# A decoder layer on one core: x is transposed unscaled and its row factors multiply each projection; the recurrence's group norm is applied on ScalarE

## The chip, the cores and the metric
The kernel runs on one core of a Trainium2 chip. A core has five engines that each work through a queue of their own, in order: TensorE (PE, with its weight loads PEld), VectorE (DVE), ScalarE (ACT), GpSimd (POOL) and SyncE (SP, which issues DMAs here). They wait for each other by semaphores. The metric is the time of one execution in microseconds (us); lower is better.

## The reference, cut to what matters
One layer over 512 positions of 2048 channels. The first norm, the input projection and the group norm are what the change touches:

```python
h = rms_norm(x, norm_g[i])              # x / sqrt(mean(x*x) + eps) * g, per position
z = jnp.einsum('btd,dn->btn', h, w_in[i])   # r, k, v, two LoRA inputs | gate | pool input | pool gate
...
zs = zs + (token_shift(zs) - zs) * mu[i]
...
y = wkv7_scan(rh, wh, kh, vh, kk, ah)   # delta-rule recurrence over time, 16 heads of 64
y = head_group_norm(y, ln_w[i], ln_b[i])    # (y - mean) * rsqrt(var + eps) per head, then w and b
y_rwkv = (y + bonus) * silu(g_rwkv)
```

Beside it a pool group takes trailing means of its projection columns; both are joined, projected by w_out, added to x, gated by a second projection (w_pg), and normed.

## The kernel before, in words
Everything is f32, and each large product is made of three fp32r products: an operand is split into a rounded part and the rest (hi and lo: `whi`, `wlo` for weights, `hhi`, `hlo` for the normed x), and PE adds hi*hi, hi*lo and lo*hi (`mm3`, called through `mm`, L157 in the profile). Of a split, ACT makes hi by a copy and DVE makes lo by a subtraction (`wsplit`, L132 and L133; `split`, L137 and L138).

The opening (L255 to L313): x comes in four tiles of 128 positions. For each tile `stats` makes sums of squares (ACT and DVE in turns, L256 and L258), a root and a reciprocal (L262, L263), and scales the tile in place (L267, L269). Then `xt_half` transposes the tile by 128 columns on PE (L285) into a small PSUM buffer (six of them, from two pools), and evicts it twice with the norm's weight: hi on ACT (L286), lo on DVE (L287). The columns of the two LoRA inputs (`zl`) are projected at once, in two halves (`z_half`), since all else in the first head waits for them.

Then PE works through a stream of projections, 128 output columns at a time, in an order that is written out (`jobs`, `stream`): k, r, v, gate of a head, and pool units (`pool_unit`) between. Each unit is 16 x 3 products of 128x512 in one PSUM tile (`zcols`); its weights come in four chunks of four (`raw`, split by ACT and DVE). A finished k, r or v goes through the token shift (`shifted`: ACT L369, DVE L370), a gate through a silu (`silu2`), a pool input `u` is copied by ACT (L412). The stream is also the filling for the recurrence: whenever the recurrence of a pair of heads has a chain of small steps, `pump(n)` puts n products of the stream between them. PE keeps the program's order there (`pin`).

For each of 8 pairs of heads j: `decay_and_rate` makes the decay from the LoRA inputs (products pu and pa, tanh, a scan along time, two exponentials `pw` and `ipw`); `norm_key` and `scale_key` make normed keys (product `pss`, a DVE reciprocal); `prepare` makes the operands `ar` and `bk`; `scores` multiplies them (pm); `invert` solves small triangular systems; `gather` collects the chunks' operands (transposes `pbk` copied by ACT to `bkn`, L700, product pmv); `recur` steps over eight chunks: py, zs, pu (to `uv` on ACT, L797), ps, and the new state `sbd` on DVE (L809). At its end the outputs (`ysb`, 128 positions x 8 groups of 64) get their group norm: statistics, a reciprocal root by Newton steps on DVE, and eight DVE operations of 128x64 that subtract the mean and multiply (L854). `finish`, some time later, transposes them (pyt) and applies weight, bias, bonus and gate (L863). The preparation of the next pair, its `gather` included, stands between.

A scheduler decides where each engine's instructions stand in its queue; only PE's order is pinned.

Of the kernel before, what the change touches and what calls it, by code (L numbers as in the profile page):

```python
# [9 lines left out]
F32 = mybir.dt.float32  # L10
# [5 lines left out]
P = 128  # L16
T = 512
# [17 lines left out]
def trunk_kernel(ctx: ExitStack, tc: tile.TileContext, x, p, norm_g, w_in, mu, w0, w_up, a0, a_up,  # L35
# [20 lines left out]
    def load_x(tt, parts):  # L56
        xt = xp.tile([P, D], F32, name=f"xt{tt}", tag="xt")
        w_ = D // parts
        for i in range(parts):
            nc.sync.dma_start(out=xt[:, i * w_:(i + 1) * w_], in_=x[tt * P:(tt + 1) * P, i * w_:(i + 1) * w_])  # L60
        xs.append(xt)

    load_x(0, 4)
# [26 lines left out]
    nc.gpsimd.memset(seg.rearrange("p (c t) -> p c t", t=C)[:, :, 0:1], 0.0)  # L90

# [96 lines left out]
    LORD = (2, "l", "l", "l", "l", 3)  # L188
# [46 lines left out]

    for step in LORD:
        if step == "l":
            load_l()
        else:
            load_x(step, 2)  # L240
# [6 lines left out]
    WPOS, SPOS = (5, 7, 9, 11), (5, 10)  # L247

    def stats(tt, parts=2):
        w_ = D // parts  # L250
        ss = xp.tile([P, parts], F32, name=f"ss{tt}", tag="ss")
        for i in range(parts):
            cs = slice(i * w_, (i + 1) * w_)
            junk = xp.tile([P, w_], F32, name=f"junk{tt}_{i}", tag=f"junk{i % 2}", bufs=2)
            if i % 2 == 0:  # L255
                nc.scalar.activation(junk, xs[tt][:, cs], AF.Square, accum_out=ss[:, i:i + 1])  # L256
            else:
                nc.vector.scalar_tensor_tensor(junk, xs[tt][:, cs], 1.0, xs[tt][:, cs], ALU.mult, ALU.mult,  # L258
                                               accum_out=ss[:, i:i + 1])
        rs = xp.tile([P, 1], F32, name=f"rs{tt}", tag="rs")  # L260
        nc.vector.tensor_reduce(rs, ss, mybir.AxisListType.X, ALU.add)
        nc.scalar.activation(rs, rs, AF.Sqrt, bias=epsr, scale=1.0 / D)  # L262
        nc.vector.reciprocal(rs, rs)  # L263
        for i in range(4):
            cs = slice(i * D // 4, (i + 1) * D // 4)
            if i % 2 == 1:
                nc.scalar.activation(xs[tt][:, cs], xs[tt][:, cs], AF.Copy, scale=rs)  # L267
            else:
                nc.vector.tensor_scalar(xs[tt][:, cs], xs[tt][:, cs], rs, None, ALU.mult)  # L269

    stats(0, 4)
# [3 lines left out]
    stats(1, 4)  # L275
# [19 lines left out]
    wl_ = []  # L295
    for d in range(KT):
        xt_half(0, d)
        if d in WPOS:
# [5 lines left out]
        if d in SPOS:  # L304
            stats(2 + SPOS.index(d))
# [875 lines left out]
```

## Time and profile before

| | us |
|---|---|
| three runs | 1095.40, 1096.56, 1097.19; median 1096.56 |
| span of the profiled execution | 1095.9, 0.66 below the median |
| PE busy | 1070.8 |
| DVE busy | 708.2 |
| ACT busy | 448.3 |
| first product of k0 (end of the opening) | starts at 35.83 |
| first scores, pm(0) | start at 75.47 |

The durations of the profile are those of single instructions; since an engine begins the next one before the last has ended, the time that each one costs in a dense row is the distance from start to start, which is shorter. A row of a timeline can hold several like instructions (x4); its length is then that of the whole run. "Idle before <-" names what ended an idle time.

### The profile page before, as it was taken

How to read it: one execution, taken by the hardware profiler on the slowest of the kernel's cores; microseconds unless marked ns; L12 is line 12 of the kernel's file. 1: busy time of each engine (PE TensorE's matmuls, PEld its weight loads, DVE VectorE, ACT ScalarE, POOL GpSimd, SP SyncE). 2: the span in 40 equal slices, each digit the busy share in tenths (PEclk: the TensorE clock that was granted, in tenths of full speed). 3: DMA queues.
4: the chain of work that ended last, by engine and by line, in shares of the span. 5: the costliest groups of instructions: out<-in, count | busy, mean ns of one | idle time of the engine just before them, and what ended most of it. 6: DMA issues, size and time to landing. Idle time of an engine off the chain costs nothing.

```text
span 1095.9 us, 17196 instructions
## 1 busy us (share of the span) xinstructions
PE 1070.8 (98%) x6060; PEld 877.6 (80%) x6060; DVE 708.2 (65%) x1835; ACT 448.3 (41%) x917; POOL 76.9 (7%) x180
## 2 busy tenths in 40 slices
PE   5999999999999999999999999999999999999996
PEld 4888878887788888788878788888888888888885
DVE  6687867878688679678886956454433424445366
ACT  7633535345335335353343344543222222233337
POOL 2100110110110110100101101000000000000000
PEclk9999999999999999999999999999999999999999
DMA  7433433332423333333334242775534438455534
GB/s 233 116 96 97 111 92 84 96 100 73 120 82 105 104 92 89 96 82 93 91 94 119 79 138 93 232 233 169 172 124 136 167 99 244 137 189 137 181 106 154
DMA packets 178486, 138.56 MB, mean 126 GB/s; under 512 B 34678, under 2 KB 139743, under 8 KB 178399
## 3 DMA queue, kind: packets, MB, share of 16 engines
q1 hardware_dynamic: 157694, 103.89, 32.1%
q10 hardware_dynamic: 20704, 33.56, 9.8%
q8 instruction: 48, 0.79, 0.3%
q14 instruction: 40, 0.32, 0.1%
HBM read 118.02 MB, written 18.87 MB: 125 GB/s over the span
## 4 chain that ended last, share of the span: by engine, by line
PE 86%; DVE 5%; DMA 4%; ACT 3%; issue 1%; SPq 0%; ACTq 0%; DVEq 0%
PE acc_o L157 16%; PE zb L157 14%; PE acc_g L157 14%; PE zv L157 8%; PE zk L157 7%; PE zg L157 7%; PE zr L157 7%; PE py L157 2%; PE pple L157 2%; PE pm L157 1%; PE pu L157 1%; DMA n<-nd 1%; PE pp L157 1%; DMA raw_g<-in_w_pg_dram 1%; PE ps L157 1%
## 5 line engine op out<-in xcount | busy, mean ns | idle before, releaser
L133 DVE TENSOR_TENSOR wlo_g<-raw_g,whi_g 128x512 fp32r<-128x512 f32 x84 | 57.0, 685 | 79.6 <-ACT whi_g L132 76.5
L157 PE MATMUL zb<-hhi,whi_b 128*128 128x512 f32 x256 | 107.0, 418 | 0.0
L133 DVE TENSOR_TENSOR wlo_o<-raw_o,whi_o 128x512 fp32r<-128x512 f32 x64 | 43.9, 690 | 91.4 <-ACT whi_o L132 91.4
L157 PE MATMUL zb<-hhi,wlo_b 128*128 128x512 f32 x256 | 100.5, 393 | 0.0
L157 PE MATMUL acc_o<-whi_o,ylo 128*128 128x512 f32 x256 | 100.2, 391 | 0.0
L157 PE MATMUL acc_o<-whi_o,yhi 128*128 128x512 f32 x256 | 99.9, 390 | 0.0
L157 PE MATMUL zb<-hlo,whi_b 128*128 128x512 f32 x256 | 99.9, 390 | 0.0
L157 PE MATMUL acc_o<-wlo_o,yhi 128*128 128x512 f32 x256 | 99.8, 390 | 0.0
L132 ACT CAST whi_g<-raw_g 128x512 fp32r<-128x512 f32 x84 | 51.9, 620 | 102.7 <-PE acc_g L157 55.4
L157 PE MATMUL acc_g<-whi_g,x2hi 128*128 128x512 f32 x208 | 81.3, 391 | 0.0
L157 PE MATMUL acc_g<-wlo_g,x2hi 128*128 128x512 f32 x208 | 80.9, 389 | 0.0
L157 PE MATMUL acc_g<-whi_g,x2lo 128*128 128x512 f32 x208 | 80.7, 389 | 0.0
L132 ACT CAST whi_o<-raw_o 128x512 fp32r<-128x512 f32 x64 | 39.9, 623 | 97.0 <-PE acc_o L157 96.7
L816 POOL TENSOR_SCALAR s0p<-sbd,pw 64x64 f32<-64x64 f32 x96 | 56.6, 589 | 322.8 <-DVE sbd L809 255.0
L132 ACT CAST whi_b<-raw_b 128x512 fp32r<-128x512 f32 x64 | 39.7, 621 | 86.5 <-PE zv L157 35.4
L133 DVE TENSOR_TENSOR wlo_b<-raw_b,whi_b 128x512 fp32r<-128x512 f32 x64 | 43.8, 685 | 34.2 <-ACT whi_b L132 32.9
L157 PEld LDWEIGHTS zb<-hhi,wlo_b 128*128 128x128 f32 x256 | 48.0, 188 | 11.1
L661 DVE TENSOR_TENSOR xw<-xw,tm 128x60 f32<-128x60 f32 (+24 forms) x248 | 52.1, 210 | 6.8
L157 PEld LDWEIGHTS acc_o<-wlo_o,yhi 128*128 128x128 f32 x256 | 48.1, 188 | 10.3 <-DVE wlo_o L133 0.4
L157 PEld LDWEIGHTS acc_o<-whi_o,yhi 128*128 128x128 f32 x256 | 48.1, 188 | 9.7
L157 PEld LDWEIGHTS acc_o<-whi_o,ylo 128*128 128x128 f32 x256 | 48.1, 188 | 9.8
L157 PEld LDWEIGHTS zb<-hhi,whi_b 128*128 128x128 f32 x256 | 48.2, 188 | 8.5
(285 smaller groups left out, 2550.0 us busy)
## 6 DMA issues: line engine op xcount, KB each, us to landing
raw_b<-in_w_in_dram SPq DMA_DIRECT2D x64, 256.0 KB
raw_o<-in_w_out_dram SPq DMA_DIRECT2D x64, 256.0 KB
raw_g<-in_w_pg_dram SPq DMA_DIRECT2D x64, 256.0 KB
raw_k<-in_w_in_dram SPq DMA_DIRECT2D x32, 256.0 KB
raw_r<-in_w_in_dram SPq DMA_DIRECT2D x32, 256.0 KB
raw_v<-in_w_in_dram SPq DMA_DIRECT2D x32, 256.0 KB
raw_g<-in_w_in_dram SPq DMA_DIRECT2D x32, 256.0 KB
n<-nd SPq DMA_DIRECT2D x16, 256.0 KB
```

The costliest lines, as they stand in the source:

```text
L132: nc.scalar.copy(hi, raw)
L133: nc.vector.tensor_tensor(lo, raw, hi.bitcast(F32), ALU.subtract)
L157: i = nc.tensor.matmul(*a, **k)
L661: nc.vector.tensor_tensor(xw[:, 0:n_, s + 1:32], xw[:, 0:n_, s + 1:32], tm[:, 0:n_, 0:w_], ALU.add)
L816: nc.gpsimd.tensor_scalar(s0p[hc, :], nxt[hc, hc], pcn[hc], None, ALU.mult)
```

## The change
1. x's tiles are loaded in another order (0 and 1 in turns, then 2 and 3 in halves between the LoRA weights) and transposed as they are. `hhi` and `hlo` hold x times the norm's weight, without the row factor. The squares come later in the program; after the first two chunks of k0's projection (24 products, now ahead of all else) `roots` makes the 512 row factors, spreads them over all partitions by a product of a matrix of ones with four diagonal matrices, `prs`, and keeps them as `rsB` (128x512).
2. Every finished projection is multiplied by `rsB`: a DVE operation in PSUM (`by_row`) for k, r, v, the gates and `zl`; for `u` the product takes the place of ACT's copy.
3. In `decay_and_rate` the lower halves of the two LoRA products use the tiles `uhh` and `ahh` (whose lower halves now hold the rest of the split), so that the ACT casts into `uaz` and the tile `lal` go.
4. The group norm is applied on ACT, eight Identity activations with scale and bias from memory; DVE makes the bias (-mean * factor) in one small operation.

The core of the diff:

```diff
-    load_x(1, 4)
+    load_x(1, 0)
+    for i in range(1, 4):
+        for tt in range(2):
+            load_x(tt, i)
...
-    LORD = (2, "l", "l", "l", "l", 3)
+    LORD = ("l", 2, 3, "l", 2, 3, "l", "l")
...
-        for i in range(4):
-            cs = slice(i * D // 4, (i + 1) * D // 4)
-            if i % 2 == 1:
-                nc.scalar.activation(xs[tt][:, cs], xs[tt][:, cs], AF.Copy, scale=rs)
-            else:
-                nc.vector.tensor_scalar(xs[tt][:, cs], xs[tt][:, cs], rs, None, ALU.mult)
...
+    def roots():
+        rs = xp.tile([P, NT, 1], F32, name="rs", bufs=1)
+        nc.vector.tensor_reduce(rs, ssq_, mybir.AxisListType.X, ALU.add)
+        nc.scalar.activation(rs, rs, AF.Sqrt, bias=epsr, scale=1.0 / D)
+        nc.vector.reciprocal(rs, rs)
+        dg = xp.tile([P, NT, P], F32, name="dg", bufs=1)
+        for tt in range(NT):
+            nc.vector.tensor_scalar(dg[:, tt, :], ident, rs[:, tt, :], None, ALU.mult)
+        ps = psM.tile([P, T], F32, name="prs", tag="m")
+        mm(ps, ones, dg.rearrange("p a t -> p (a t)"), start=True, stop=True)
+        nc.scalar.copy(rsB, ps)
...
     for d in range(KT):
         z_half(1, d)
+        if d % CK == CK - 1 and d < 3 * CK:
+            ahead_k()
+        square(d // 4, d % 4)
+    pin[0] = True
+    begun = psA.tile([P, T], F32, name="zk0", tag="acc")
+    for c in range(BEGUN):
+        k_first(c)
+    roots()
...
+    nc.vector.tensor_tensor(zl, zl, rsB, ALU.mult)
     shifted(zl, la, 24)
...
+    def by_row(ps):
+        nc.vector.tensor_tensor(ps, ps, rsB, ALU.mult)
...
+                if kk == KT - 1 and scaled:
+                    by_row(ps)
                 yield 3
...
-            nc.scalar.copy(u_, ps)
+            nc.vector.tensor_tensor(u_, ps, rsB, ALU.mult)
...
-            nc.scalar.copy(z_[hi, :], raw[hi, :])
-            nc.vector.tensor_tensor(st[lo, :], raw[lo, :], st[lo, :].bitcast(F32), ALU.subtract)
+            nc.vector.tensor_tensor(z_[0:64, :], raw[0:64, :], st[0:64, :].bitcast(F32), ALU.subtract)
...
-        mm(ps, uaz[0], lal, start=False, stop=True)
+        mm(ps, uaz[0], uhh, start=False, stop=True)
...
+        nc.vector.scalar_tensor_tensor(nt8, mvr[:, :, 0:1], -1.0, rs8, ALU.mult, ALU.mult)
         for i in range(8):
-            nc.vector.tensor_scalar(y8[:, i, :], y8[:, i, :], mvr[:, i, 0:1], rs8[:, i, :],
-                                    ALU.subtract, ALU.mult)
+            nc.scalar.activation(y8[:, i, :], y8[:, i, :], AF.Identity, scale=rs8[:, i, :], bias=nt8[:, i, :])
```

The change moves instructions in the queues. In the rows below each instruction has its line, its operation, what it writes and reads, and the tile's size; the lines of the changed kernel are 3 to 32 higher.

DVE's queue at the start, before, from the end of the first tile's squares to the first evictions (`junk` are the squares, `rs` the row factor, `xt` the tile of x, `hlo` the eviction):

```order
L261 TENSOR_REDUCE rs_170<-ss_161 128x1
L263 RECIPROCAL rs_170<-rs_170 128x1
L269 TENSOR_SCALAR xt_78<-xt_78,rs_170 128x512 x2
L258 SCALAR_TENSOR_TENSOR junk_1_184,ss_181<-xt_85 128x512
L86 CAST blk<-blkf 128x128
L274 COPY ngc<-pt_prm 128x16
L258 SCALAR_TENSOR_TENSOR junk_3_188,ss_181<-xt_85 128x512
L261 TENSOR_REDUCE rs_190<-ss_181 128x1
L263 RECIPROCAL rs_190<-rs_190 128x1
L269 TENSOR_SCALAR xt_85<-xt_85,rs_190 128x512 x2
L287 SCALAR_TENSOR_TENSOR hlo<-pt_h_0_199,ngc,hhi 128x256
L287 SCALAR_TENSOR_TENSOR hlo<-pt_h_1_204,ngc,hhi 128x256
```

The same place in the changed kernel:

```order
L264 SCALAR_TENSOR_TENSOR junk_1_401,ssq__164<-xt_78 128x512
L89 CAST blk<-blkf 128x128
L281 COPY ngc<-pt_prm 128x16
L264 SCALAR_TENSOR_TENSOR junk_3_417,ssq__164<-xt_78 128x512
L264 SCALAR_TENSOR_TENSOR junk_1_427,ssq__164<-xt_79 128x512
L293 SCALAR_TENSOR_TENSOR hlo<-pt_h_0_169,ngc,hhi 128x256
L293 SCALAR_TENSOR_TENSOR hlo<-pt_h_1_174,ngc,hhi 128x256
L293 SCALAR_TENSOR_TENSOR hlo<-pt_h_2_179,ngc,hhi 128x256
```

The reductions, reciprocals and scalings are gone from the head of the queue; three squares of the first two tiles are left ahead of the first `hlo`, though the program writes them later.

DVE's queue ahead of the first scores, from a weight split of the gate to the last operand `bk` (`kk` keys, `kp` the other operand, `sv` the shifted v), before:

```order
L599 TENSOR_TENSOR kk_817<-kk_817,tha_844 128x512
L133 TENSOR_TENSOR wlo_g_3_777<-raw_g_3_774,whi_g_3_776 128x512
L370 SCALAR_TENSOR_TENSOR sv_933<-zv_801,prm,sv_933 128x511
L600 TENSOR_TENSOR bk_961<-kk_817,ipw_837 128x4x128
L601 SCALAR_TENSOR_TENSOR kp_962<-sr_798,dprm,kp_962 128x512
L133 TENSOR_TENSOR wlo_k_0_783<-raw_k_0_780,whi_k_0_782 128x512
```

The same place in the changed kernel:

```order
L139 TENSOR_TENSOR wlo_g_3_783<-raw_g_3_780,whi_g_3_782 128x512
L425 TENSOR_TENSOR zv_779<-zv_779,rsB 128x512
L630 TENSOR_TENSOR kk_795<-kk_795,tha_820 128x512
L632 SCALAR_TENSOR_TENSOR kp_939<-sr_776,dprm,kp_939 128x512
L398 SCALAR_TENSOR_TENSOR sv_910<-zv_779,prm,sv_910 128x511
L139 TENSOR_TENSOR wlo_k_0_789<-raw_k_0_786,whi_k_0_788 128x512
L631 TENSOR_TENSOR bk_938<-kk_795,ipw_813 128x4x128
```

The product of zv by `rsB` is new; `kp` and the split of `wlo_k_0` stood behind `bk` and now stand ahead of it.

ACT's queue at the gather for the second pair of heads, before (`pw`, `ipw` exponentials, `bkn` the copies of the operands, `uaz` the casts, `zs`, `mv` first chunk):

```order
L539 ACTIVATE pw_2386<-sig_2382 128x8x64
L132 CAST whi_b_2_1384<-raw_b_2_1382 128x512
L540 ACTIVATE ipw_2387<-sig_2382 128x512
L700 COPY bkn_2404<-pbk_0_2405 128x512
L700 COPY bkn_2404<-pbk_1_2411 128x512
L525 CAST uaz_570<-ur_2595 64x128
L524 CAST as_2602<-ar_2599 128x128
L525 CAST uaz_571<-ar_2599 64x128
L712 COPY zs_568<-pmv_2438 64x128
L713 COPY mv_2455<-pmv_2438 128x512
```

The same place in the changed kernel, where L886 is the group norm of the pair before:

```order
L570 ACTIVATE pw_2367<-sig_2363 128x8x64
L138 CAST whi_b_2_1388<-raw_b_2_1386 128x512
L886 ACTIVATE ysb_1642<-ysb_1642,nt_2329,rs_2326 128x64 x8
L571 ACTIVATE ipw_2368<-sig_2363 128x512
L731 COPY bkn_2385<-pbk_0_2386 128x512
L731 COPY bkn_2385<-pbk_1_2392 128x512
L743 COPY zs_599<-pmv_2419 64x128
L744 COPY mv_2436<-pmv_2419 128x512
```

The eight applies stand behind `whi_b_2` and ahead of `ipw` and both `bkn`; the two `uaz` casts are gone. The sixth pair's gather has the same order; at the others one or both `bkn` stand ahead of the applies.

More of the change, by code (lines that the diff above doesn't have):

```diff
@@ L234, in load_l @@
         lraw.append(raw)
+    halves = []
     for step in LORD:
@@ L239, in trunk_kernel @@
         else:
-            load_x(step, 2)
+            load_x(step, halves.count(step), 2)
+            halves.append(step)
     for n_, src, r_ in names:
@@ L244, in trunk_kernel @@
         nc.sync.dma_start(out=prow[col[n_]:col[n_] + r_, :], in_=flat.rearrange("(r c) -> r c", c=P))
[L247 to L256, printed above, removed]
-            else:
[L258 to L261, printed above, removed]
+    WPOS = (9, 11, 13, 15)
```

76 lines of the change are left out of this document (46 added, 30 removed).

## The prediction

> **What bounds the kernel now.** I read the page first, for the busy time of each engine and the chain that ended last.
> ```profile
> PE 1070.8 (98%) x6060; PEld 877.6 (80%) x6060; DVE 708.2 (65%) x1835; ACT 448.3 (41%) x917; POOL 76.9 (7%) x180
> PE 86%; DVE 5%; DMA 4%; ACT 3%; issue 1%; SPq 0%; ACTq 0%; DVEq 0%
> ```
> TensorE (PE) is busy for 98% of the span and is 86% of the chain. DVE is 5% of the chain and ACT 3%. So work that leaves DVE or ACT gains nothing by itself; what counts is when PE begins its dense stretch and where it waits afterwards. The table by stage (columns: stretch, its length, busy time of PE, PEld, DVE, ACT and POOL, clock, DMA share, GB/s) and the list of PE's waits say where these places are.
> ```profile
> 0.00:10.00 10.00, 1.37 (x5) 0.89 (x5) 3.65 (x12) 5.11 (x12) 6.46 (x54) 1.00 0.76 238
> 10.00:20.00 10.00, 7.66 (x42) 5.96 (x43) 8.12 (x23) 8.90 (x22) 0.00 (x0) 1.00 0.90 291
> 20.00:30.00 10.00, 8.85 (x67) 7.63 (x67) 9.66 (x25) 9.77 (x24) 0.00 (x0) 1.00 0.38 110
> 30.00:40.00 10.00, 10.00 (x70) 9.29 (x69) 7.82 (x25) 5.99 (x14) 2.93 (x11) 1.00 0.36 102
> ```
> ```profile
> PE pt_prm L273 <- DMA ngr<-in_norm_g_dram: 7.1, 1, 7.1
> PE pt_h L285 <- DVE xt L269: 3.3, 2, 1.8
> PE py L157 <- DVE sbd L809: 1.6, 4, 0.9
> PE pss L157 <- ACT bkn L700: 0.9, 2, 0.5
> ```
> In the first 30 us PE idles 12.1 us: 7.1 for the first data, the rest for scaled rows of x and for DVE and ACT, both near full between 20 and 30. All later waits together come to a few microseconds. So the change can gain only in the opening, and it loses wherever it makes a new wait.
>
> **The opening.** The rows are DVE's and ACT's timelines (start, length of the whole run of instructions, their count).
> ```profile
> 10.55 0.69 DVE L258 SCALAR_TENSOR_TENSOR junk<-xt 128x512 f32<-128x512 f32 x1 [0.54 <-DMA xt<-in_x_dram]
> 11.35 0.16 DVE L261 TENSOR_REDUCE rs<-ss 128x1 f32<-128x4 f32 x1
> 12.07 0.88 DVE L269 TENSOR_SCALAR xt<-xt,rs 128x512 f32<-128x512 f32 x2
> 13.80 1.66 DVE L287 SCALAR_TENSOR_TENSOR hlo<-pt_h,ngc,hhi 128x256 fp32r<-128x256 f32 x4 [0.84 <-ACT hhi L286]
> ...
> 32.20 1.27 DVE L287 SCALAR_TENSOR_TENSOR hlo<-pt_h,ngc,hhi 128x256 fp32r<-128x256 f32 x3
> 33.38 1.28 DVE L133 TENSOR_TENSOR wlo_k<-raw_k,whi_k 128x512 fp32r<-128x512 f32 x2
> ```
> ```profile
> 35.56 0.28 PE L157 MATMUL zl<-hlo,whi_l 128*128 128x256 f32 x1
> 35.68 0.28 PE L157 MATMUL zl<-hhi,wlo_l 128*128 128x256 f32 x1
> ...
> 35.83 0.48 PE L157 MATMUL zk<-hhi,whi_k 128*128 128x512 f32 x1
> 36.14 0.39 PE L157 MATMUL zk<-hlo,whi_k 128*128 128x512 f32 x1
> 36.37 0.40 PE L157 MATMUL zk<-hhi,wlo_k 128*128 128x512 f32 x1
> ```
> Removed from the way to the first product are root, reciprocal and scaling. The squares are written later in the program, but in the compiled order three of DVE's and four of ACT's still stand ahead of the first eviction. The last of DVE's three comes behind the seventh of the eight x pieces; the eighth of before landed at 10.53 (0.54 of waiting ended by the row at 10.55), so the seventh is put at 9.9, an estimate. Two squares at 0.70 apart end at 11.3, and hlo begins there instead of 13.80. Successive hlo start 0.40 apart ((1.27-0.48)/2) and successive 128x512 splits 0.60 ((1.28-0.68)/1). DVE's queue is then 32 x 0.40 + 4 x 0.60 = 15.2 us, without stalls until 26.5. The last pair of transposes needs the buffer that the hlo six units earlier frees, 24.1, and I add 1.1 for ACT's squares between its evictions: 25.2. Behind it lie 48 zl products 0.12 apart, 5.8 us: k0 begins at 31.0 instead of 35.83, **-4.8**. Bounds: -6.3 (PE's 142 instructions behind the third hlo at 12.5, none slower than 0.12, done back to back by 29.5) and -3.5 (the 48 products begin only behind the last hlo, 26.5 + 5.8 = 32.3).
>
> Five of DVE's squares now run while PE does zl and the first 24 products of k0 (24 x 0.23 = 5.5 us, to 36.5). DVE ends the last hlo at 26.5, then 4 splits and 5 squares (5.9), then reduce, root, reciprocal (0.7 from the rows at 11.35 and 12.07) and four small products: about 34.6. So the roots are ready ahead of PE, and cost nothing; if that cover fails, PE waits at prs. The product prs itself, f32 128x512, has no row; one fp32r product takes 0.23, four are 0.9. I take **+0.45**.
>
> **The first block.** The keys for the first scores are made on DVE, in one queue without idle time.
> ```profile
> 62.11 3.33 DVE L572 RECIPROCAL kk<-kk 128x512 f32<-128x512 f32 x1
> 65.35 1.22 DVE L133 TENSOR_TENSOR wlo_g<-raw_g,whi_g 128x512 fp32r<-128x512 f32 x2
> ...
> 72.89 0.68 DVE L600 TENSOR_TENSOR bk<-kk,ipw 128x512 f32<-128x512 f32 x1
> ```
> ```profile
> 75.47 0.71 PE L157 MATMUL pm<-ar,bk 64*128 64x128 f32 x8
> ```
> Before, bk ends at 73.57, 1.9 us ahead of pm: covered. The reciprocal began 26.28 behind k0's first product (62.11 - 35.83). After, that is 31.0 + 26.28 + 0.45 for prs = 57.7, and the product of zr by rsB now stands between PE and the shift of r that ACT and DVE make ahead of the reciprocal: 0.60 and one more handing over, I take 1.1, so 58.8, 3.3 earlier than before. From its start to the end of bk it was 11.46 us; three instructions are now ahead of bk that were not: zv by rsB (0.60), kp (0.65) and one split (0.60). That is 1.9 more: 58.8 + 11.46 + 1.9 = 72.2. PE would be there at 75.47 - 4.8 + 0.45 = 71.1. So the cover is gone, and pm waits 1.1: of the opening's 4.8, **3.2** are left (bounds 2.0, if zl, zk and zr cost twice as much and the reciprocal begins at 60.0, and 4.4, if bk is in time).
>
> **The norm on ACT.** Eight applies on DVE become eight on ACT, and at two of the seven gathers they stand ahead of ipw and of the copies bkn. The next rows are ACT's and then PE's timeline at the first such place, and the two that matter at the second.
> ```profile
> 187.58 0.63 ACT L539 ACTIVATE pw<-sig 128x512 f32<-128x512 f32 x1 [0.57 <-DVE rs L151]
> 188.12 0.60 ACT L132 CAST whi_b<-raw_b 128x512 fp32r<-128x512 f32 x1
> 188.63 0.62 ACT L540 ACTIVATE ipw<-sig 128x512 f32<-128x512 f32 x1
> 189.27 1.07 ACT L700 COPY bkn<-pbk 128x512 f32<-128x512 f32 x2
> ```
> ```profile
> 188.31 1.15 PE L157 MATMUL pmv<-uv,mt 64*64 64x64 f32 x32
> 189.90 0.50 PE L157 MATMUL pss<-kqh,blk 128*128 128x512 f32 x1 [0.45 <-ACT bkn L700]
> ```
> ```profile
> 489.14 1.07 ACT L700 COPY bkn<-pbk 128x512 f32<-128x512 f32 x2
> ```
> ```profile
> 489.78 0.50 PE L157 MATMUL pss<-kqh,blk 128*128 128x512 f32 x1 [0.46 <-ACT bkn L700]
> ```
> ACT runs without a gap from pw to bkn; PE already waits 0.45 and 0.46 for the first bkn, and it takes its work in order, so whatever ACT puts ahead of bkn is lost in full. What one apply costs, I work out from these groups (the last columns: count, busy us, mean ns).
> ```profile
> L797 ACT COPY uv<-pu 64x64 f32<-64x64 f32 x102 | 21.0, 206 | 39.1 <-PE pu L157 38.3
> L700 ACT COPY bkn<-pbk 128x512 f32<-128x512 f32 x14 | 7.6, 588 | 0.1
> L863 ACT ACTIVATE yo<-pyt,dprm 128x512 f32<-128x512 f32 x6 | 4.7, 778 | 8.4 <-PE pyt L161 8.4
> ```
> A copy of 64 columns takes 0.206. An Identity with a scale and a bias read from memory takes 0.19 more than a copy of the same size (0.778 against 0.588). Two successive copies overlap by 0.11 (2 x 0.588 - 1.07). So 0.206 + 0.19 - 0.11 = 0.29, I take 0.30 and eight are 2.4; the ends are 0.206 (1.65) and 0.40 without overlap (3.2). Two places: **+4.8** (3.3 to 6.3). At the other gathers bkn stands ahead of the applies or a wait of PE has other cover, so nothing is charged but 0.3 for the transposes pyt of the norm's output.
>
> In the Trainium skill, "ScalarE: Activation LUTs", section "What ACT_TABLE_LOAD costs", an activation is 186 ns and 0.833 ns per column, each operand read from memory adds 93 ns, and back-to-back ones overlap by 93 ns. By that page one apply would be an estimated 0.33 us and two places 5.3 instead of 4.8; the step from copy to yo agrees with it (0.190 against 0.186).
>
> **The row factor.** Forty finished projections, the eight u (whose ACT copies go) and zl get a DVE product of 128x512 from PSUM; put at the splits' 0.60 that is 49 x 0.60 = 29 us of DVE, which has 388 us idle. Behind each finished projection ACT's shift waits for the product; nobody waits for that shift at once. But in DVE's queue zg, zk and zr stand ahead of a state update sbd, for which py and ps wait; PE has 9 products (2.1 us) between, which is the cover. Where it is thin already (py on sbd, 1.6 us in four waits) I charge **+0.5** (0 to 1.5). The 16 casts of the LoRA halves that go from ACT lie on no wait.
>
> **Sum.** -3.2 + 4.8 + 0.3 + 0.5 = +2.4. The profiled execution took 1095.9; that makes 1098.3. The median of the runs shown is 0.66 above that span, so 1099.0 is forecast. 0.2%, 2.2 us, is about what a measurement of this kernel can tell from no change; the forecast is just outside.
>
> **Rivals.**
> A, faster: the applies cost next to nothing at pss. Place: the two rows of pss above. The profile infers releasers from semaphores, and pss also starts right behind pmv (end 189.46); if PE stands there for pmv's drain, and ACT's bkn only ends at the same time, then 4.8 goes. Both rows show the same 0.45, and the releaser ends 0.05 before PE starts, which speaks against it. It decides from a price of 0.15 per apply downward, where the sum turns negative. Then -3.2 + 0.8 = -2.4: 1094.2. With bk in time as well it is 1093.0.
> In the Trainium skill, "ScalarE: Activation LUTs", section "Rules for kernel authors", multiplications and additions belong on VectorE. By that rule the move can only lose; in this trace that would hold where PE waits for ACT, as it does at the two rows of pss.
>
> B, slower still: nothing of the opening's gain is left. The change would not do what it says, since squares are still ahead of the first evictions and the roots come late: if rsB is 0.9 later than I put it, r0 waits for the buffer of zl, and the reciprocal moves with it. Then pm stands at its old time, and the sum is 0 + 4.8 + 0.8 = +5.6: 1102.2. Against it: 1.9 us between roots and prs.
>
> C, slower: the row factors in DVE's queue delay the state updates in every head. One 0.60 per head more in each of 8 heads is +4.8, the sum +7.2: 1103.8. For it: PE waits for sbd already in four places; against: 9 products of cover.
>
> **Chances.** Forecast 0.46, A 0.30, B 0.12, C 0.12. A's weight is for all that could hide a wait of ACT and that I can't see in an order. The forecast's own range, its terms at their lower and upper ends (-4.4 + 3.3 and -2.0 + 6.3 + 0.3 + 1.5), is 1095.5 to 1102.7; a little more than half of it lies above 1098.8, nearly all the rest within 0.2%. Faster: 0.24 of A and 0.02, 0.26. Same: 0.06 of A and 0.20, 0.26. Slower: 0.24 and B and C, 0.48. The range runs from 1093.0 (A with bk in time) to 1103.0, which leaves out half of C and little of A.
>
> **What would show it.** Right: k0 begins near 31; pm(0) near 72.3 with a wait for DVE's bk of about 1; ACT rows of the norm with 0.4 us each between whi_b and ipw; two pss waits for bkn near 2.9 instead of 0.45; PE otherwise as busy. Wrong, if those two waits stay under 1 us (A), if k0 begins after 33 or prs waits (B), or if the waits for sbd grow beyond 3 us in all (C).

## The result, and the profile after

The changed kernel took 1114.46 us (median of 4 runs, 1113.09 to 1118.55), the kernel before 1096.55 (median of 4, 1095.4 to 1097.19). The ratio is 1.0164 (95% interval 1.0143 to 1.0186): 1.6% slower, some 18 us. Forecast were 1099.0 with a range up to 1103.0, so the sign was right and the size far off: the profiled span grew by 15.4 us (1095.9 to 1111.4) where the sum had 2.4. The profiled execution is the shortest of the four (1113.09), so the span shows less than the whole loss.

The page after has TensorE's (PE's) busy time and the shares of the chain that ended last.
```profile
PE 1077.1 (97%) x6062; PEld 880.7 (79%) x6062; DVE 721.4 (65%) x1822; ACT 457.2 (41%) x951; POOL 70.0 (6%) x181
...
PE 75%; DVE 9%; DMA 7%; ACT 4%; issue 3%; ACTq 0%; SPq 0%; DVEq 0%
```
Two things can be read there. PE's share of the chain fell from 86% to 75%, so waits were added. And PE is busy 6.3 us longer (1077.1 against 1070.8) with only two instructions more: some of its work ran slower. The list of PE's waits after (total us, times, longest) says where the first part is.
```profile
PE pss L163 <- ACT bkn L731: 6.1, 3, 2.9
...
PE py L163 <- DVE sbd L840: 4.2, 6, 1.6
...
PE pyt L167 <- ACT ysb L886: 2.3, 7, 0.3
PE pu L163 <- DVE zs L818: 1.3, 3, 0.7
```
The wait for `bkn` is the one that was forecast (0.9 before). `pyt` is not in the list of before at all, and `pu` stands there with one wait of 0.4. The table by stage after, ten microseconds each, shows the second part: these are the only two such stretches of the dense part in which the granted clock (the third number from the end) is below 1.00.
```profile
190.00:200.00 10.00, 7.34 (x27) 5.91 (x28) 7.68 (x10) 7.17 (x16) 0.00 (x0) 0.83 0.20 58
500.00:510.00 10.00, 9.83 (x66) 7.83 (x67) 8.56 (x12) 4.30 (x10) 0.00 (x0) 0.83 0.10 28
```

**Where the span went.** Waits and modelled durations overlap, so I also divided each span among PE's instructions: the time from one instruction's start to the next one's, booked to the tile of the second (for `prs`, which is new, to the tile of the first). The differences to before, in us:

| tile | forecast | after | norm on DVE again (first experiment) | before with only the norm moved (second) |
|---|---|---|---|---|
| up to `k0`'s first product | -4.8 | -3.2 | -2.0 | +0.7 |
| `prs` | +0.45 | +0.9 | +0.9 | none |
| `pss` | +4.8 | +5.5 | -0.1 | +5.5 |
| `zv`, `zb`, `zg` (the products behind `pss` are among them) | 0 | +3.2 | +0.1 | +3.0 |
| `pyt` | +0.3 | +4.1 | +0.2 | +0.6 |
| `py` | +0.5 with `pu` | +2.3 | +3.0 | +3.3 |
| `pu` | | +2.2 | +2.4 | +0.4 |
| whole span | +2.4 | +15.4 | +6.5 | +13.9 |

What the rows leave out is spread over other tiles; the largest is `acc_o`, +1.1 in the changed kernel and +1.8 in the last column. The profiled executions of the last two columns are 1.8 and 3.6 us longer than the medians of their runs, so the columns serve to compare places; the times below are what the parts cost.

**The gather for the second pair of heads.** ACT's timeline after, then PE's (start, length, idle time before and its releaser):
```profile
188.72 2.75 ACT L886 ACTIVATE ysb<-ysb,nt,rs 128x64 f32<-128x64 f32 x8
191.39 0.61 ACT L571 ACTIVATE ipw<-sig 128x512 f32<-128x512 f32 x1
192.03 0.59 ACT L731 COPY bkn<-pbk 128x512 f32<-128x512 f32 x1
```
```profile
192.66 0.54 PE L163 MATMUL pss<-kqh,blk 128*128 128x512 f32 x1 [2.86 <-ACT bkn L731]
193.00 0.63 PE L163 MATMUL pss<-kql,blk 128*128 128x512 f32 x1
193.43 0.63 PE L163 MATMUL zv<-hhi,whi_v 128*128 128x512 f32 x1
...
195.99 0.59 PE L163 MATMUL zb<-hhi,whi_b 128*128 128x512 f32 x1
196.41 0.39 PE L163 MATMUL zb<-hlo,whi_b 128*128 128x512 f32 x1
```
The eight applies stand where the order of the queues had them, and PE's wait grew from 0.45 to 2.86. Behind the wait the products start 0.43 apart for 3.4 us (193.00 to 196.41), and only then 0.23 apart as everywhere else. The finer table of the same place after shows the granted clock with it:
```profile
194.00:196.00 2.00, 2.00 (x7) 1.52 (x6) 1.13 (x3) 0.38 (x2) 0.00 (x0) 0.50 0.00 0
196.00:198.00 2.00, 2.00 (x12) 1.65 (x10) 1.74 (x3) 1.11 (x2) 0.00 (x0) 0.90 0.06 16
```
Eight products 0.20 longer each make 1.6 us a place, 3.2 at two: a cost that the prediction did not have, and half of PE's longer busy time. (In the first experiment, without slow products, PE is still busy 3.7 us longer than before.)

**The transposes of the norm's output.** PE's timeline after, behind the next gather:
```profile
271.56 0.54 PE L167 MATMUL pyt<-ident,ysb 128*128 128x128 f32 x2
272.44 0.33 PE L167 MATMUL pyt<-ident,ysb 128*128 128x128 f32 x1 [0.34 <-ACT ysb L886]
273.10 0.33 PE L167 MATMUL pyt<-ident,ysb 128*128 128x128 f32 x1 [0.34 <-ACT ysb L886]
```
Each transpose needs two applies, which ACT gives every 0.66 us (twice 0.33, the pitch of the row of eight above); the four transposes start over 1.54 us. With the applies on DVE the four stand in one run and the next product starts 0.56 us behind the first (the first experiment, its PE timeline):
```profile
270.33 0.81 PE L167 MATMUL pyt<-ident,ysb 128*128 128x128 f32 x4
270.89 0.48 PE L163 MATMUL zb<-hhi,whi_b 128*128 128x512 f32 x1
```

### The profile page after: what moved, and what is told of

The parts are those of the page before. It is cut to its first block, busy times and chain, and to the rows that moved or that the text cites. A ratio compares the mean times of both kernels' runs of the same rounds, so it can differ in the third digit from the quotient of the medians.

```text
span 1111.4 us, 17219 instructions
## 1 busy us (share of the span) xinstructions
PE 1077.1 (97%) x6062; PEld 880.7 (79%) x6062; DVE 721.4 (65%) x1822; ACT 457.2 (41%) x951; POOL 70.0 (6%) x181
## 4 chain that ended last, share of the span: by engine, by line
PE 75%; DVE 9%; DMA 7%; ACT 4%; issue 3%; ACTq 0%; SPq 0%; DVEq 0%
PE acc_g L163 15%; PE acc_o L163 15%; PE zb L163 11%; PE zv L163 7%; PE zr L163 6%; PE zg L163 6%; PE zk L163 5%; DMA n<-nd 3%; PE pple L163 2%; PE py L163 2%; PE pu L163 1%; ACT ysb L886 1%; DMA xt<-in_x_dram 1%; DMA yin<-yd 1%; DVE tm L688 1%
## 5 line engine op out<-in xcount | busy, mean ns | idle before, releaser
L847 POOL TENSOR_SCALAR s0p<-sbd,pw 64x64 f32<-64x64 f32 x96 | 52.8, 550 | 333.8 <-DVE sbd L840 266.0
```

What stands on the lines that cost most here:

```text
L847: nc.gpsimd.tensor_scalar(s0p[hc, :], nxt[hc, hc], pcn[hc], None, ALU.mult)
```

## The experiments

The theory formed on seeing the result had three separate parts: the norm on ACT costs 11 to 12 us (wait for `bkn`, halved clock behind it, waits of `pyt`), the row factor 6 to 8, and the opening gives some 2 back. The rivals: the norm's waits only show because the row factor has made ACT late; or the row factor's operations are covered and the opening lost its gain somewhere else; or the slow products have nothing to do with the wait ahead of them. The kernels before in the comparisons took 1096.99 to 1098.26 us.

**1. The norm on DVE again, the rest of the change kept.**
```diff
-        nc.vector.scalar_tensor_tensor(nt8, mvr[:, :, 0:1], -1.0, rs8, ALU.mult, ALU.mult)
...
-            nc.scalar.activation(y8[:, i, :], y8[:, i, :], AF.Identity, scale=rs8[:, i, :], bias=nt8[:, i, :])
+            nc.vector.tensor_scalar(y8[:, i, :], y8[:, i, :], mvr[:, i, 0:1], rs8[:, i, :],
+                                    ALU.subtract, ALU.mult)
```


> The changed kernel with the eight applies of the norm back on DVE; all else as changed. Theory S (most of the loss hangs on the applies on ACT): the two waits of pss for bkn (2.86 each), the slow products behind them (9 at 0.43 instead of 0.23, clock 0.50, 1.6 us at each) and the waits of pyt for ysb (4.05 in all) go, 5.3 + 3.3 + 4.05 = 12.6 of the 17.9: about 1102. Rival D (the row factors' 49 products on DVE are the loss, the applies only stand where it shows): DVE gets 15 us more work back, so the time stays above 1108.

Measured: 1102.36 against 1098.26, ratio 1.0041 (1.0026 to 1.0056). Its waits:
```profile
PE py L163 <- DVE sbd L840: 4.5, 6, 1.8
...
PE pu L163 <- DVE zs L818: 1.3, 3, 0.7
PE pss L163 <- ACT bkn L731: 0.8, 3, 0.4
```
The wait for `bkn` is back at 0.8, the slow products and the waits of `pyt` are gone. Three quarters of the loss belong to the norm. What is left, 0.41% or 4.1 us, is still slower than before, so the rest of the change loses too.

**2. Only the norm moved, in the kernel before** (the same edit the other way round).

> The kernel before, with only the applies of the norm moved to ACT. Theory S: the loss comes with this part alone, pss waits near 2.9 at the second and sixth gather, the clock falls to 0.50 behind them, pyt waits: 1096.5 + 12.6 = about 1109. Rival D: without the row factors ACT's delay stays below 5 us: 1098 to 1101, and the granted clock stays at 1.00.

Measured: 1108.31, ratio 1.0100 (1.0084 to 1.0116). The list of its waits has, for `pss`:
```profile
PE pss L157 <- ACT bkn L700: 6.2, 2, 3.1
```
The norm alone makes the wait for `bkn`, and slow products follow at both places, here not at once but 0.8 and 1.5 us behind the wait's end (waits of 3.12 and 3.11, slow from 195.25 and 502.57); the clock is 0.83 in the same two stretches of ten microseconds. So the row factor is not what makes ACT late there, and the first rival falls. `pyt` lost only 0.6 here; with the row factor it is 4.1.

**3. Every second apply on ACT, the others on DVE.**
```diff
+            if i % 2 == 0:
                 nc.scalar.activation(y8[:, i, :], y8[:, i, :], AF.Identity, scale=rs8[:, i, :], bias=nt8[:, i, :])
+            else:
+                nc.vector.tensor_scalar(y8[:, i, :], y8[:, i, :], mvr[:, i, 0:1], rs8[:, i, :],
+                                        ALU.subtract, ALU.mult)
```


> The changed kernel with every second apply on ACT and every second on DVE: half the dose. Theory S with a threshold in the clock: pss waits 0.45 + 1.3 = 1.8 at the two gathers, the clock behind them stays at 1.00 since the idle time is shorter, and pyt's waits fall to about 1 in all: 1114.5 - 2.6 - 3.3 - 3 = about 1105.5. Rival L (the slow products go with the idle time in proportion): half of the 1.6 us is left at each place, some 4 products at 0.43: about 1107.

Measured: 1104.53, ratio 1.0052 (1.0037 to 1.0066). Its wait for `bkn`, and the stretch behind the first one:
```profile
PE pss L163 <- ACT bkn L731: 3.5, 3, 1.5
```
```profile
194.00:196.00 2.00, 2.00 (x9) 1.66 (x10) 1.95 (x4) 1.57 (x5) 0.00 (x0) 1.00 0.50 142
```
PE stands up to 1.5 us here, and the clock stays at 1.00 (0.50 in the same stretch after). `pss` lost 2.6, half of 5.5, but the slow products lost only 0.1: the wait goes by the number of applies, the clock by some threshold. It is not a length of the wait alone: in this kernel PE also waits 2.66 for `sbd` (until 154.09), and no slow product follows.

**4. Twelve products of the stream ahead of `pss`.** All eight applies stay on ACT; PE gets 2.8 us of other work in front of the wait.
```diff
+        pump(12)
...
-        pump(H5)
+        pump(H5 - 12)
```


> The changed kernel with 12 of the 13 stream products that follow pss at a gather put ahead of it: the applies stay on ACT, but PE has 2.7 us of work while they run. Theory S: the waits of pss fall from 2.86 to below 0.5, and with them the slow clock goes: 5 + 3.3 = 8 us less, about 1106.5; the waits of pyt stay. Rival: the slow products have another cause than PE's idle time (the burst of small pmv products ahead of it, which stays): the clock still falls behind pss, and only 5 us are gained, about 1109.5.

Measured: 1107.64, ratio 1.0091 (1.0077 to 1.0104). Its PE timeline at the same gather:
```profile
192.89 0.50 PE L163 MATMUL pss<-kqh,blk 128*128 128x512 f32 x1 [0.43 <-ACT bkn L731]
193.23 0.40 PE L163 MATMUL pss<-kql,blk 128*128 128x512 f32 x1
```
ACT does the same work, but the wait is 0.43 and the second product already takes the usual 0.40. That makes the wait, and not ACT's work in itself, the cause of the slow products; some 7 us of span come back (1111.4 to 1104.5), a little less than the 8.5 of `pss` and the slow products, while another tile, `pq`, lost 1.9. The waits of `pyt` stay: +3.8.

**5. The first experiment without the row products of k, r, v and the gates.** This leaves out that part of the computation.
```diff
-    def zcols(ps, nm, scaled=True):
+    def zcols(ps, nm, scaled=False):
```


> The applies on DVE, and the row factors' products for k, r, v and the gates left out (only zl and the pool inputs are still multiplied); the opening stays as changed. Theory P (the products in DVE's queue delay sbd and zs, which PE waits for): the 5.4 us that py and pu cost more fall to about 1, and with the opening's gain kept the kernel comes to 3 us under the kernel before with the norm on DVE, about 5 less than that one: 1097, level with before. Rival N (the opening's gain is eaten because the DMA of n for the second pair lands at a fixed time, and the later waits are bad luck of phase): py and pu stay above 3, and the time above 1100.

Measured: 1095.14 against 1098.13, ratio 0.9977 (0.9968 to 0.9986). This is the only kernel in the study that was faster than before, by 3.0 us, and it leaves work out: it is about what the opening gives. Beside the first experiment (1.0041) the 40 row products of these projections cost 0.64%, 7 us. Its waits:
```profile
PE py L163 <- DVE sbd L840: 4.3, 7, 1.7
...
PE pu L163 <- DVE zs L818: 0.6, 2, 0.4
```
`pu` is at 0.6 instead of 1.3; `py` is not. So the waits of `py` are no mark of the row factor: `py` took about 3 us more than before here, in the first experiment and in the second, which has no row factor at all.

**6. Only a row product, in the kernel before.** The factor is a mask that is already in memory, whose zeros change what is computed.
```diff
+    nc.vector.tensor_tensor(zl, zl, seg, ALU.mult)
...
+                if kk == KT - 1 and scaled:
+                    nc.vector.tensor_tensor(ps, ps, seg, ALU.mult)
...
-            nc.scalar.copy(u_, ps)
+            nc.vector.tensor_tensor(u_, ps, seg, ALU.mult)
```


> The kernel before with nothing but the 49 products of 128x512 on DVE: each finished projection is multiplied by a mask that lies in memory already (its zeros change what is computed, not the work). Theory P: py and pu cost 4 to 6 us more and the first scores may come late: 1098.3 + 5 = about 1103. Rival N: without the earlier start PE meets no new wait: within 2 us of before.

Measured: 1105.51, ratio 1.0070 (1.0057 to 1.0083). With no new opening and the norm on DVE, 49 products cost 0.70%, which agrees with the 0.64% of the step from 5 to 1. The parts nearly add up: norm 1.00%, row factor 0.70%, opening -0.23% make 1.47%, the whole change 1.64%. The 0.17% (1.9 us) between is within what the intervals allow; it would also fit `pyt`, which lost 4.1 with norm and row factor together and 0.6 with either alone. Its ACT timeline shows a second way in which the product costs:
```profile
110.66 0.69 ACT L369 ACTIVATE sr<-zr,dprm 128x512 f32<-128x512 f32 x1 [4.65 <-DVE zr L405]
```
Before, the same shift starts at 105.74 right behind a cast of ACT, with no wait. Now ACT stands for 4.65 us at the head of its queue until DVE has multiplied `zr`.

**7. Six of eight applies on ACT**, to find the threshold; all else as in number 3.
```diff
+            if i % 4 < 3:
```


> The changed kernel with six of eight applies on ACT and two on DVE: the dose between half (no slow products) and all (9 slow products at two places). The waits of pss should be 0.45 + 6 x 0.32 = 2.3 each. If the clock needs an idle time near 2.9 us, products behind stay at 0.23 and the kernel is 1104.5 + 1.5 = about 1106.5. If any idle time over 2 us is enough, the slow products come back and it is about 1109.5.

Measured: 1108.21, ratio 1.0089 (1.0073 to 1.0105). Its PE timeline at the two gathers:
```profile
194.96 0.74 PE L163 MATMUL pss<-kqh,blk 128*128 128x512 f32 x1 [2.20 <-ACT bkn L731]
195.50 0.63 PE L163 MATMUL pss<-kql,blk 128*128 128x512 f32 x1
195.93 0.63 PE L163 MATMUL zv<-hhi,whi_v 128*128 128x512 f32 x1
...
502.94 0.50 PE L163 MATMUL pss<-kqh,blk 128*128 128x512 f32 x1 [2.29 <-ACT bkn L731]
503.28 0.40 PE L163 MATMUL pss<-kql,blk 128*128 128x512 f32 x1
```
After 2.20 us the products are slow, after 2.29 they are not. In the same kernel waits of 2.15 (until 153.08) and 1.99 (until 460.73) for `sbd` are followed by slow products too. So it is not the length of a wait that decides; what does is worked out below. (The profiled execution is the longest of four here, 1112.85, and has three such places; its mean clock is 0.993, that of the other three 0.995 to 0.997.)

**8. More cover in front of `pu`,** on the first experiment: eight products of the stream between `zs` and `pu` instead of six, eight instead of nine at the two other steps.
```diff
-    HC, HT, HX = (6, 9, 9), 130, 13
+    HC, HT, HX = (8, 8, 8), 130, 13
```


> The applies on DVE, and the products that fill a step of the recurrence dealt out as 8, 8, 8 instead of 6, 9, 9: two more behind py, where DVE has to make zs, one less each for uv and sbd. Theory P: the waits of pu for zs (1.3 us and more) go, those of py for sbd grow by 0.23 at each place where they exist: 0 to 2 us less than 6, 9, 9, which took 1102.4. If the waits come from ACT or DMA instead, nothing changes but more waits for sbd: 1103 to 1106.

Measured: 1107.8, ratio 1.0084 (1.0069 to 1.0099), slower than the first experiment. `pu` fell from +2.4 to -2.0 against before, but `py`, with one product less in front, rose from +3.0 to +7.0 and `pyt` to +4.8; behind a wait of `py` (1.91, until 152.94) the clock fell once, from 153.21. So `pu` does wait for cover, and there is none to spare beside it.

**9. The opening of before, with three of four scalings of x's second half on GpSimd.**
```diff
+            if tt >= 2 and i >= 1:
+                nc.gpsimd.tensor_scalar(xs[tt][:, cs], xs[tt][:, cs], rs, None, ALU.mult)
...
```


> The kernel before with one thing moved in the opening: three of four scalings of the third and the fourth tile of x go from ACT and DVE to GpSimd, which is idle there. DVE is near full between 20 and 30 us, and loses 2 of these products at 0.44, ACT 4 at 0.61. If DVE's and ACT's queues set the start of k0, it comes 0.9 to 2 us earlier and the kernel is 0 to 2 us faster, 1096.2 to 1098; if GpSimd's products are slow (589 ns for 64x64 in the recurrence), the transposes of these tiles wait for them and k0 begins 2 to 6 us later.

Measured: 1096.45 against 1096.99, ratio 0.9993 (0.9980 to 1.0005): no difference. `k0` began 0.46 us earlier. Taking only these scalings from DVE and ACT gives nothing that the time shows.

**10. The row product written behind the head's step,** on the first experiment: it is issued after the last `zs` or `sbd` on DVE.
```diff
-                    by_row(ps)
...
+            with tc.issue_after(last[0].ins):
+                by_row(ps)
```


> The changed kernel with the norm's applies on DVE and each row product told to stand behind the last zs or sbd in DVE's queue instead of ahead of the next one; the amount of work is the same. Theory P (the place in the queue is what costs): py and pu together cost 2 us or less more than before, instead of 5.4, so some 3 to 4 us less than with the applies on DVE alone (1102.4, +4.1 on its chip): level with before, -1 to +1.5. Rival W (DVE's added work as such, 29 us, costs, wherever it stands: weight splits and the shifts come late): the same +4, within 1 us.

Measured: 1101.04 against 1096.99, ratio 1.0038 (1.0025 to 1.0051). `pu` lost 1.1 instead of 2.4, but in time the kernel loses what the first experiment lost (0.38% against 0.41%). ACT's standing in front of the shift is not shorter (4.76 us at 110.09), and everything behind it on ACT still waits.

**11 and 12. The shift's first half on DVE,** so that ACT waits for no row product; number 11 on number 10, number 12 on the first experiment.
```diff
-        nc.scalar.activation(dst, ps, AF.Copy, scale=dp(0, mi))
+        nc.vector.tensor_scalar(dst, ps, dp(0, mi), None, ALU.mult)
```


> The applies on DVE, each row product behind the last zs or sbd, and the first half of the token shift moved from ACT to DVE (a tensor-scalar product of 128x512), so that ACT has nothing in its queue that waits for a row product of r, k or v. Theory H (the row products cost in two ways: ahead of sbd and zs in DVE's queue, and through ACT's queue, which stands still behind the shift, 4.76 us at 110 in the version before, with sig, bkn and q behind it): pbk, pss and px lose their waits, some 3 us less than with the product behind alone, near 1098 and level with before. Rival W (the added DVE work as such): 14 us more work on DVE, so 1 to 3 us slower than with the product behind alone.

> The applies on DVE and the shift's first half on DVE, the row products where the changed kernel has them. Theory H: pbk, pss and px lose their waits (some 3 us), py and pu keep theirs or get 1 us more: 1 to 3 us below the version with the applies on DVE alone. Rival W: 1 to 3 us above it.

Measured: 1109.5 (1.0102, 1.0082 to 1.0121) and 1112.69 (1.0130, 1.0108 to 1.0151). The waits of number 11:
```profile
PE pyt L167 <- DVE ysb L890: 4.5, 1, 4.5
...
PE pss L163 <- ACT bkn L736: 3.0, 3, 2.6
```
The waits of `px` and `pbk` (1.4 and 0.6 us in the first experiment's list) are gone. But one transposition stands 4.5 us for a norm apply on DVE, and `pss` 2.6 for a `bkn` on ACT. DVE's timeline at the first of these:
```profile
348.37 3.35 DVE L608 RECIPROCAL kk<-kk 128x512 f32<-128x512 f32 x1
351.63 1.78 DVE L890 TENSOR_SCALAR ysb<-ysb,mvr,rs 128x64 f32<-128x64 f32 x8
```
The long reciprocal of the keys stands ahead of the eight applies; in the first experiment the applies (343.87) stood ahead of it (347.78). Number 12 has the same order there and the same 4.5. As a cure both kernels miss, and by far more than either theory had. The three places where number 11 loses most against number 10, `pyt` (5.5), slow products behind long waits (3.6) and `pss` (2.2), make 11.3 us, where the two spans differ by 10.5. So added work also changed the order of DVE's queue, and one instruction of 3.35 us in the wrong place cost more than ACT's standing. What the added work costs by itself these two kernels don't show.

**13 and 14. The first and the tenth again, side by side.** No edit.

> The applies on DVE alone, once more, on the chip of the three others, as the point to compare them with: before + 4.1, as in its first run.

> The row products behind the last zs or sbd, once more, on the same chip as the applies on DVE alone. Theory H: only the part of py and pu goes, 1 to 3 us below the applies on DVE alone. Rival W: level with it, as the medians of the two jobs had it.

Measured against 1098.07: 1103.11 (1.0044, 1.0027 to 1.0062) and 1101.41 (1.0028, 1.0012 to 1.0044). The later place in the queue is 1.7 us better, by the medians; the intervals overlap, and numbers 1 and 10 lost the same, so the 1.7 are not shown. `pu` again lost 1.0 instead of 2.4. No version with the whole computation was measurably faster than the kernel before.

## Why the prediction was wrong in size

Three steps of the prediction failed. The sum had no term for what PE's clock does behind a wait (3.2 us). "Nothing is charged but 0.3 for the transposes" was 4.1. And the row factor, charged at 0.5 because nine products stand in front and "nobody waits for that shift at once", cost about 7.

**What bounds the kernel** was right: PE's waits, and what ACT or DVE do only where PE waits for them. The direction followed from that: the wait at `pss` alone outweighs the opening.

**The opening: -4.8 for `k0`, -3.2 kept; measured -3.2 and -2.3.** `hlo` was to begin at 11.3. DVE's timeline after:
```profile
10.65 0.69 DVE L264 SCALAR_TENSOR_TENSOR junk<-xt 128x512 f32<-128x512 f32 x1 [3.06 <-DMA xt<-in_x_dram]
...
11.88 1.26 DVE L293 SCALAR_TENSOR_TENSOR hlo<-pt_h,ngc,hhi 128x256 fp32r<-128x256 f32 x3
...
21.62 0.69 DVE L144 TENSOR_TENSOR wlo_l<-raw_l,whi_l 128x512 fp32r<-128x512 f32 x1 [0.95 <-ACT whi_l L143]
```
The piece that two squares wait for landed later than the 9.9 put for it, so `hlo` began at 11.88. DVE's queue was taken to run without stalls; it stood 0.95 here and 0.36 once before (at 17.63) for ACT's half of a weight split. `k0` then began at 32.59 instead of 31.0, just beyond the bound of 32.3. PE's timeline after, at the roots and at the first block:
```profile
38.06 1.02 PE L163 MATMUL prs<-dg,ones 128*128 128x512 f32 x2
38.92 0.24 PE L167 MATMUL pt_prm<-ident,prow 89*128 89x89 f32 x1
...
73.15 0.72 PE L163 MATMUL pm<-ar,bk 64*128 64x128 f32 x8
```
`prs` appears as two instructions, and the next one starts 0.86 behind it: twice the 0.45 taken. `pm` shows no wait for `bk` where 1.1 was forecast: the key chain was in time. So errors of both signs left 75.47 - 73.15 = 2.3 of the 3.2. In the time this fits the 3.0 us of experiment 5. The start of `k0` differs by over 2 us between kernels with the same opening (-1.1 to -3.3 against before), so the opening's share can't be had closer than that.

**The norm at `pss`: +4.8, measured +5.5.** Mechanism and place were right, at both gathers. The two waits were forecast near 2.9 and are 2.86; a third gather, where none was forecast, has one of 0.38. An apply starts 0.33 behind the one before, (2.75 - 0.44) / 7 with 0.44 for the first one's length, not 0.30. The Trainium skill, "ScalarE: Activation LUTs", section "What ACT_TABLE_LOAD costs", gives the price from which 0.33 and 5.3 were estimated in the prediction; the trace agrees with it, better than with my own sum.

**What no step had: the clock behind the wait, 3.2.** The prediction counted a wait of 2.9 as 2.9. It costs 4.5, because eight products follow at half speed. Experiment 4 shows that it is the wait, 2 that it needs nothing else of the change. The Trainium skill, "TensorE: Matmul & The Clock Gate", section "What's actually happening", has a clock that halves after one idle window of about 3.4 us, in windows that run freely, and that recovers after as long. The recovery agrees (3.4 us), and so do the windows. The stretches at 0.50 in the changed kernel begin at 192.99 and 500.19, 307.20 apart, 90 times 3.413; in each of the six traces in which the clock changed in the dense part the changes stand whole multiples of 3.413 us apart, wherever the waits fall, and against the kernel's start they lie differently from trace to trace (the clock's record begins at 15.4 to 18.8 us of the span). What differs is that a window need not be idle throughout. Counted window by window over all 16 traces, the clock fell behind each of the ten windows in which PE idled 1.91 us or more, behind two of the four with 1.82 to 1.90, and behind none with 1.75 or less. This settles the 2.29 us of experiment 7. The window's line, and the next one's, with PE's busy time behind the length:
```profile
498.83:502.24 3.41, 1.82 (x36) 1.28 (x34) 3.41 (x9) 3.41 (x9) 0.00 (x0) 1.00 0.04 8
502.24:505.66 3.42, 2.72 (x12) 2.24 (x13) 3.32 (x7) 2.78 (x7) 0.00 (x0) 1.00 0.26 74
```
The boundary at 502.24 divides the wait into 1.59 and 0.70, and the clock stays at 1.00; the wait of 2.20 at the other place lies in one window (191.62 to 195.04) and costs the next one. The 2.66 of experiment 3 is divided too, into 1.90 and 0.76.

**"Nothing is charged but 0.3 for the transposes": +4.1.** The step that failed is the sentence that at the other gathers a wait of PE has other cover. It looked at when the applies stand against `bkn`, not at the rate at which they feed `pyt`: two applies of 0.33 for each transposition against a stretch of PE that takes them all in 0.56. With the norm back on DVE it was +0.2 (1), with the norm on ACT and `pss` cured +3.8 (4). But in experiment 2, with the norm on ACT and no row factor, the same transposes lost only 0.6. So the pitch costs where the applies also come late, and the row products make them late: at the gather shown above the first apply starts 3.7 us ahead of the first transposition before, 3.4 in experiment 2 and 3.7 in 5, which have no products of k, r, v and gates, but 1.8 in 1 and 6 and 1.6 in the changed kernel, which have them. The lateness comes from DVE, whose queue makes the norm's factors; on ACT, at 0.33 or more an apply, it shows, and on DVE, at 0.22 to 0.32, mostly not.

**The row factor: +0.5, measured about 7** (0.64% from 5 to 1, 0.70% in 6). Rival C, 4.8, was nearer, and had a chance of 0.12, but by luck: it saw the loss in waits for `sbd`. These did grow beyond its mark of 3 us, to 4.2, yet they are 4.4 and 4.3 in experiments 2 and 5, without these products. Two sentences failed. One put nine products of cover in front of DVE's steps; that holds for `py` and `ps`, but between `zs` and `pu` there are six. DVE's and PE's timelines at such a place after:
```profile
398.35 0.70 DVE L425 TENSOR_TENSOR zr<-zr,rsB 128x512 f32<-128x512 f32 x1
398.96 0.68 DVE L139 TENSOR_TENSOR wlo_v<-raw_v,whi_v 128x512 fp32r<-128x512 f32 x1
399.56 0.28 DVE L818 TENSOR_TENSOR zs<-py,mv 64x128 f32<-64x128 f32 x1
```
```profile
399.89 0.49 PE L163 MATMUL pu<-zs,x 128*128 128x128 f32 x2 [0.72 <-DVE zs L818]
```
The product and a split stand ahead of `zs`, and PE waits 0.72. `pu` lost 2.0 to 2.6 in the changed kernel and in experiments 1, 3, 4, 6, 7 and 13, all with the products in this place; 1.0 to 1.1 with the products behind (10, 14); and 0.4 and -0.3 without them (2, 5). The other sentence was "nobody waits for that shift at once". True of the shift itself; what is queued behind it on ACT was not looked at. ACT's timeline after:
```profile
107.81 0.69 ACT L397 ACTIVATE sr<-zr,dprm 128x512 f32<-128x512 f32 x1 [4.28 <-DVE zr L425]
...
109.10 0.69 ACT L563 ACTIVATE sig<-pu,dprm 128x512 f32<-128x512 f32 x1
```
`sig`, on which the next pair's operands and with them `pbk` and `bkn` depend, stands behind the shift. In the lists of waits `pbk`, which waits for `sig`, and `px` stand with 0.6 and 1.4 us in the first experiment, 0.2 and 0.8 here, and not at all in number 11, where this wait of ACT is gone. For `px` the profile names no releaser; the copy of `q`, which ACT ends 0.1 us ahead of it, stands behind the next shift.

**The waits of `py`** are another matter. `py` lost 1.4 us or more in every kernel of the study but number 9, with row products and without. At the second pair in the changed kernel the loss comes from a transfer that does not move with PE. DVE's timelines, before and after:
```profile
147.90 0.19 DVE L657 TENSOR_TENSOR tm<-i,n 128x31 f32<-128x31 f32 x1 [2.33 <-DMA n<-nd]
```
```profile
148.02 0.19 DVE L688 TENSOR_TENSOR tm<-i,n 128x31 f32<-128x31 f32 x1 [3.73 <-DMA n<-nd]
```
The data comes at the same time though PE is 1.2 us earlier; DVE then has the product of `zg` (0.70) and `sbd` to do, and PE waits 1.59 for it. A part of the opening's gain is lost there. The other places are alike: in the changed kernel each of the five longest waits of `py` (4.0 of its 4.2 us) ends 3.5 to 4.1 us behind the end of such a wait of DVE for `n`, and so do the four longest in the first experiment and the three longest in the sixth. Why the transfer comes late for PE there also without an earlier start (experiments 2 and 6) was not separated.

**What stays open.** How the 7 us divide. From number 5 to number 1 the spans differ by 7.0: `pu` has 2.7 of it, `px` 1.4, `pss` and `pbk` 0.9, the start of `k0` 1.3, which differs between like kernels anyway, and `py` nothing; the rest is small. How much of it is the place of the products in DVE's queue and how much their length was not separated: with the later place `pu` lost 1.4 less, but the time did not measurably change.

**The sum again.** Of the 13.0 us by which the span missed the sum, 3.8 are `pyt` (4.1 for 0.3), 3.2 the clock, 4.2 `py`, `pu`, `px` and `pbk` (4.7 for the 0.5 charged to the row factor, though `py`'s 2.3 of it are not its), 0.9 the opening and 0.7 `pss`; the rest is small and of both signs. The range was built from the ends of the terms named, so a cost without a term could not be in it.

## What to carry to other kernels

Where an instruction gets a new operand from another engine, list what stands behind it in its own queue, and who waits for that, before calling the wait harmless; and for work put into a queue, count the smallest cover in front of any consumer, not the usual one. A wait that idles PE for about 1.9 us within one window of 3.41 us may cost up to 1.6 us more than its length, so it is worth moving independent products ahead of it. The windows do not start with the kernel, so the same wait can cost this in one execution and not in another; the mean clock of experiment 7's four runs is 0.993 to 0.997. An engine that is idle for a third of the span, as DVE is here, can still be what PE waits for in the stretches that count: 0.6 us each for 49 operations, 29 us against 388 idle, cost 7.

## What the runs showed of the hardware that was not expected

- TensorE's granted clock changed only at multiples of a window of 3.413 us, which runs by itself. Behind a window in which PE idled 1.91 us or more it fell to 0.50 for the next one (ten of ten; once it stayed there for two); with 1.75 or less it never fell. 128x512 products then started 0.43 apart instead of 0.23. A wait of 2.66 us that a boundary divided left the clock alone; one of 1.83 within a window (number 12) halved it.
- A product of f32 operands (`prs`, 128x512) appears as two instructions and took 0.86 us, nearly four times the 0.23 of an fp32r product.
- In the profiled execution of experiment 5 the granted clock reads 0.95 throughout, with products still 0.23 apart. A reading slightly below 1 did not show in their spacing; 0.50 did.
